# A two-layer decoder trunk: loads of the weight sums queued at other places, accumulation banks exchanged, early squares on ScalarE

## The chip, the cores and the metric

The kernel runs as one program on one core of a Trainium2 chip. The metric is the device time of one execution in microseconds (us). A core has a matrix engine (TensorE; PE in the profile, its weight loads PEld), a vector engine (VectorE; DVE), a scalar engine (ScalarE; ACT), a general engine (GpSimd; POOL), and an engine that mostly issues transfers (SyncE; SP). Each works through a queue of its own in order; where one needs another's result its instruction waits on a semaphore, and all that stands behind it in that queue waits too. SBUF is the on-chip memory. PSUM holds the results of matmuls, in banks that another engine must copy out before PE can write them again.

## The reference

The input is 1024 positions by 1024 features in float32. Two layers follow one another; each adds an attention block and an MLP to the stream. Cut to what matters:

```python
for i in range(DEPTH):                       # DEPTH = 2
    hn = rmsnorm(x, attn_norm_g[i])
    if i % 2 == 0:
        mix, q_cross = mla_mixer(hn, positions, ...)      # 12 heads, low-rank q and kv
    else:
        mix, q_cross = swa_mixer(hn, positions, ...)      # window of 128, 12 heads
    cross = memory_cross_attention(q_cross, mem_n, w_mem_kv[i])   # 4 heads
    x = x + jnp.concatenate([mix, cross], axis=-1) @ w_o[i]
    x = x + squared_relu_mlp(rmsnorm(x, mlp_norm_g[i]), mlp_w_up[i], mlp_w_down[i])
return rmsnorm(x, final_norm_g)

def squared_relu_mlp(h, w_up, w_down):
    a = jax.nn.relu(h @ w_up)
    return (a * a) @ w_down
```

## The kernel before

**Products.** Every large product is made from float32 numbers split in two: `split` (L96 to L104) has ACT round a tile to its high part `hi` (L99, or L103 with a gain) and DVE subtract it for the low part `lo` (L100, or L104). A product is then three matmuls, high by high, high by low and low by high. The output projections and the MLP also use a seven-product scheme on 2 by 2 blocks: sums of blocks are multiplied, in the products p = 1 to 7, in place of eight block products. So DVE and ACT have splits and block sums to make while PE multiplies.

**The order.** The program is written as one long function whose stages run through generators; `next(...)` advances one of them by a step at a place chosen by hand. A scheduler then orders each engine's queue within that frame, and pools of SBUF hand memory on: a tile that gets memory of an earlier tile waits for its last users. SP's queue carries nearly all transfers, so a transfer waits for those ahead of it too.

**The weight sums.** `wo_sums` (L594) makes, for a layer, sums of the blocks of `w_o` that products 5, 7, 6 and 4 of its output projection need, and stores them in DRAM (`wt_5h`, `wt_5l` and so on). The unit is a set n of four 128 by 256 tiles, of which there are eight a layer. `load(n)` issues the loads; four instructions on DVE (L620 to L623) make the sums in place; `put` splits one sum (L99, L100) and stores high and low part (L610). `run` is the generator, with two steps a set; `step` is the number of sets that have buffers. In layer 0 the first four sets use one set of buffers; sets 4 to 7 use the pool `wop` with 24 tiles: four sets of four, and eight tiles for high parts. All their loads are issued at once (L695), and the sums run in the loop over t that makes the values (`values_of`, L701) and, through `crossing`, the cross attention. `wop` is released (L831) before the tiles of the first heads are opened (`hb`, with the constant rows `kh` and `kl` that POOL writes in `head_ones`, L754 and L755), and before the loop over j that makes the keys (`pskn`) and the loads `wr` of the query weights (L526). In layer 1 two sets have buffers (tile `f1`, named `fb` in the trace), the high parts lie in query tiles (`q1`), and the sums run in the jobs n = 4 to 9 that make the queries. Directly after the last job's sums the first window scores (`s_qk`, L2062) use `f1` again.

**Cross attention.** Its scores are `pscx` (L376), maxima are taken on DVE (L423), the exponentials on ACT (L425, tile `cps`), reciprocals on DVE (L426), scaling on POOL (L428); PE transposes (`pscT`, L388), DVE and ACT copy (L392, L394), and PE multiplies (`psco`, L403).

**The output projection.** `wo_phase` (L1218) runs products 1, 5, 6, 3, 2, 7, 4 in four steps each on two groups of four banks, Y (`pswy`) and Z (`pswz`). One group is made of two double banks (`ps2`), the other of four single ones (`ps1`). In layer 0 the last attention head's result `pso` is still in PSUM when it begins, and ACT copies it out (L1032).

**The MLP.** `mlp` (L1425 on) makes the hidden blocks. `load_raw` loads a block row i of the up weights in two halves (tiles `mr` or `d`, L1443), ACT scales them (L1416), DVE makes block sums (L1459 to L1462), `prep_w` and `prep_x` split weights and input, PE multiplies (`psu`, `psv`, L1520 to L1522). `evac` copies out: for products 2, 7 and 3 DVE adds a saved product (L1572) and `square` makes relu(a)·a in one DVE instruction (L1551); sums of the squared blocks follow (L1582 to L1584), and `write` stores them. `xT_` transposes the input (`psT_m`, L1345) while the first rows i = 0 and 1 begin.

## Time and profile before

| | us |
|---|---|
| median of 3 runs | 2135.39 |
| lowest, highest | 2134.42, 2136.19 |
| the profiled execution, its own time | 2133.98 |
| its span in the profile | 2131.8 |

| stage, us from the start of the span | length | PE busy | DVE busy | ACT busy |
|---|---|---|---|---|
| 0 to 206: norms, input products, cross attention, first sums | 206 | 185.53 | 144.73 | 115.09 |
| 206 to 455: queries, layer 0's heads | 249 | 246.41 | 190.56 | 172.17 |
| 455 to 545: layer 0's output projection | 90 | 87.51 | 70.64 | 63.34 |
| 545 to 1128: layer 0's MLP | 583 | 574.32 | 419.69 | 271.97 |
| 1128 to 1345: layer 1's input products, cross attention, sums | 217 | 205.75 | 138.77 | 108.36 |
| 1345 to 1505: layer 1's windows and output projection | 160 | 158.94 | 135.24 | 129.51 |
| 1505 to 2131: layer 1's MLP, last norm | 626 | 611.34 | 447.74 | 289.02 |

The profile is of one execution, read by a hardware profiler. Its times are counted from the start of the span. A row of the timeline reads: start, duration, engine, line, operation, tiles written and read, shapes, and in brackets the time for which the engine was idle before it, and the instruction that ended this. Rows with x2 or more are runs of equal instructions put together. A row of the windows reads: the stretch and its length, then busy time and number of instructions of PE, PEld, DVE, ACT and POOL, the TensorE clock that was granted as a share of full speed (PEclk), the busy share of the DMA engines and GB/s. SPq rows are SP's issues of transfers. Times of PE overlap a little, as matmuls are pipelined: what counts there is the distance from start to start.

### The profile page before, as it was taken

The page shows a single profiled execution, that of the slowest core. Times are in us where ns is not written, and L with a number is a line of the kernel's source. Part 1 is how long each engine was busy: PE and PEld are TensorE (multiplying, and loading weights), DVE is VectorE, ACT ScalarE, POOL GpSimd, SP SyncE. Part 2 cuts the span into 40 slices and gives each one's busy share as a digit, 9 for nine tenths or more (in the row PEclk, how much of TensorE's full clock was granted, in tenths as well). Part 3 has the DMA queues.
Part 4 walks back from the last instruction along what each step waited for, and adds up shares of the span by engine and source line. Part 5 has one row for each costly group of instructions (what it writes and reads, how often), then busy time and mean ns, then how long its engine had stood idle before and what let it go on. Part 6 is the DMA issues. An engine that isn't in the chain of part 4 may idle for free.

```text
span 2131.8 us, 29731 instructions
## 1 busy us (share of the span) xinstructions
PE 2069.8 (97%) x9832; PEld 1691.2 (79%) x9832; DVE 1547.4 (73%) x3011; ACT 1149.5 (54%) x2504; POOL 163.6 (8%) x224
## 2 busy tenths in 40 slices
PE   7999999999999999999999998999999999999998
PEld 6887778778778888788888876778788878788887
DVE  7667688876977776886557557797987776976565
ACT  5556477867754453444445544777754443444452
POOL 0003100001000000000001241531000000000000
PEclk9999999999999999999999999999999999999999
DMA  8523224257254446954433226137254446954442
GB/s 268 163 62 117 60 61 120 69 164 244 84 174 150 144 142 213 324 170 144 148 119 94 75 77 207 44 121 260 89 168 163 142 132 226 324 160 152 120 119 89
DMA packets 209796, 314.43 MB, mean 147 GB/s; under 512 B 21629, under 2 KB 101994, under 8 KB 209642
## 3 DMA queue, kind: packets, MB, share of 16 engines
q1 hardware_dynamic: 196960, 293.63, 43.2%
q0 software_dynamic: 4016, 13.12, 1.8%
q10 hardware_dynamic: 8666, 5.80, 0.9%
q8 instruction: 77, 1.26, 0.3%
q14 instruction: 77, 0.63, 0.1%
HBM read 206.34 MB, written 93.63 MB: 141 GB/s over the span
## 4 chain that ended last, share of the span: by engine, by line
PE 67%; DMA 11%; DVE 11%; ACT 5%; issue 3%; SPq 1%; POOL 1%; DVEq 0%; ACTq 0%; POOLq 0%
PE psy L1857 5%; PE psy L1859 5%; PE psy L1858 5%; PE psz L1858 4%; PE psz L1859 4%; PE psz L1857 4%; DMA mr<-in_mlp_w_up_dram 4%; PE pss L947 4%; PE pso L989 4%; DMA d<-in_mlp_w_up_dram 3%; PE psu L1520 3%; PE psu L1522 2%; PE psu L1521 2%; PE psv L1522 1%; PE psv L1521 1%
## 5 line engine op out<-in xcount | busy, mean ns | idle before, releaser
L1416 ACT ACTIVATE mr<-mr,gcol 128x256 f32<-128x256 f32 (+1 forms) x160 | 68.0, 480 | 80.7 <-DMA mr<-in_mlp_w_up_dram 69.2
L1416 ACT ACTIVATE d<-d,gcol 128x256 f32<-128x256 f32 x128 | 57.8, 500 | 87.4 <-DMA d<-in_mlp_w_up_dram 73.8
L1857 PE MATMUL psy<-g 128*128 128x512 f32 x256 | 99.9, 390 | 0.0
L1858 PE MATMUL psy<-g 128*128 128x512 f32 x256 | 99.6, 389 | 0.0
L1859 PE MATMUL psy<-g 128*128 128x512 f32 x256 | 99.3, 389 | 0.0
L99 ACT ACTIVATE g<-i 128x512 fp32r<-128x512 f32 x79 | 49.6, 628 | 88.2 <-PE psz L1858 45.4
L100 DVE TENSOR_TENSOR g<-i,g 128x512 fp32r<-128x512 f32 x79 | 55.8, 706 | 50.1 <-ACT g L99 50.0
L99 ACT ACTIVATE uh<-i 128x512 fp32r<-128x512 f32 x66 | 41.6, 631 | 86.4 <-PE psy L1858 40.7
L968 ACT ACTIVATE p<-pss 128x512 f32<-128x512 f32 x108 | 63.6, 593 | 42.6 <-PE pss L947 42.1
L99 ACT ACTIVATE i<-mr 128x512 fp32r<-128x512 f32 x78 | 49.0, 629 | 69.5 <-PE psz L1858 20.4
L100 DVE TENSOR_TENSOR pl<-p,ph 128x512 fp32r<-128x512 f32 (+1 forms) x96 | 61.7, 652 | 25.6 <-ACT ph L99 25.0
L821 DVE TENSOR_REDUCE m<-psx 128x1 f32<-128x128 f32 (+5 forms) x96 | 70.3, 749 | 11.3 <-PE psx L817 11.1
L100 DVE TENSOR_TENSOR uh<-i,uh 128x512 fp32r<-128x512 f32 x66 | 45.5, 690 | 45.3 <-ACT uh L99 45.2
L1857 PE MATMUL psz<-g 128*128 128x512 f32 x192 | 74.7, 389 | 0.0
L1858 PE MATMUL psz<-g 128*128 128x512 f32 x192 | 74.7, 389 | 0.0
L1859 PE MATMUL psz<-g 128*128 128x512 f32 x192 | 74.7, 389 | 0.0
L100 DVE TENSOR_TENSOR i<-mr,i 128x512 fp32r<-128x512 f32 x78 | 53.6, 687 | 22.0 <-ACT i L99 21.6
L99 ACT ACTIVATE ph<-p 128x512 fp32r<-128x512 f32 (+1 forms) x96 | 56.4, 599 | 1.3
L1859 PEld LDWEIGHTS psy<-g 128*128 128x128 f32 x256 | 48.1, 188 | 10.0
L1857 PEld LDWEIGHTS psy<-g 128*128 128x128 f32 x256 | 48.1, 188 | 9.9
L1738 DVE TENSOR_TENSOR mqf<-mqq,mqf 128x512 f32<-128x512 f32 x64 | 43.1, 686 | 17.7 <-DMA mqq<-in_mlp_w_down_dram 17.5
L1858 PEld LDWEIGHTS psy<-g 128*128 128x128 f32 x256 | 48.1, 188 | 9.9
(709 smaller groups left out, 6984.5 us busy)
## 6 DMA issues: line engine op xcount, KB each, us to landing
i<-hd SPq DMA_DIRECT2D x154, 256.0 KB
hd<-uh SPq DMA_DIRECT2D x76, 256.0 KB
hd<-ul SPq DMA_DIRECT2D x76, 256.0 KB
mr<-in_mlp_w_up_dram SPq DMA_DIRECT2D x36, 512.0 KB
hd<-x SPq DMA_DIRECT2D x72, 256.0 KB
mr<-hd SPq DMA_DIRECT2D x70, 256.0 KB
d<-in_mlp_w_up_dram SPq DMA_DIRECT2D x32, 512.0 KB
mqq<-in_mlp_w_down_dram SPq DMA_DIRECT2D x32, 512.0 KB
```

What stands on the lines that cost most here:

```text
L99: r = nc.scalar.activation(hi, src, AF.Copy)
L100: nc.vector.tensor_tensor(lo, src, f32(hi), ALU.subtract)
L821: nc.vector.reduce_max(m8s[h][:, i : i + 1], ps[:, c], axis=AX, negate=True)
L947: return lambda: nc.tensor.matmul(o, a, b, skip_group_check=True, **kw)
L989: mms.append(lambda: nc.tensor.matmul(o, a, b, skip_group_check=True, **kw))
L1416: nc.scalar.activation(w[:, k, :], w[:, k, :], AF.Copy, scale=g_mlp[layer][:, k0 + k : k0 + k + 1])
L1520: nc.tensor.matmul(ps, wh[:, k, :], xh[:, k, :], start=p in (1, 2, 5) and k == 0, stop=False, skip_group_check=True)
L1521: nc.tensor.matmul(ps, wh[:, k, :], xl[:, k, :], start=False, stop=False, skip_group_check=True)
L1522: nc.tensor.matmul(ps, wl[:, k, :], xh[:, k, :], start=False, stop=k == 3, skip_group_check=True)
L1857: nc.tensor.matmul(ps, ah[:, j, :], bh, start=p in (1, 5, 2) and k == 0, stop=False, skip_group_check=True)
L1858: nc.tensor.matmul(ps, ah[:, j, :], bl, start=False, stop=False, skip_group_check=True)
L1859: nc.tensor.matmul(ps, al[:, j, :], bh, start=False, stop=k == NP - 1, skip_group_check=True)
```

## The change

It has six parts.

1. `run` of the weight sums: with more than one set of buffers, the next set's loads are issued at the start of the next set's sums instead of after the last `put`.
2. Layer 0's second half: the pool `wop` moves to the other side of SBUF and shrinks to 10 tiles, two sets of buffers and two tiles for high parts. The steps come at t = 1 and 2 and then once per j in the loop over the keys, and the pool is released after that loop.
3. `wo_phase` in layer 0: Z gets its double banks first, then Y its single ones.
4. `prep_x`: two splits of 128 columns become one of 256, where both are due together.
5. `square` of the rows i = 0 and 1: Relu and then Square on ACT, in place of the one instruction on DVE.
6. Layer 1: the sums' first loads are issued at job 3 instead of 4.

```diff
@@ -616,6 +616,8 @@
             if step == 1:
                 yield
             for n in ns:
+                if step > 1 and n > ns[0] and n - 1 + step in ns:
+                    load(n - 1 + step)
                 s = sets[n % step]
                 V(s[0], s[1], s[0], ALU.subtract)
                 V(s[1], s[2], s[1], ALU.subtract)
@@ -628,8 +630,8 @@
                 yield
                 put(n, 2)
                 put(n, 3)
-                if n + step in ns:
-                    load(n + step)
+                if step == 1 and n + 1 in ns:
+                    load(n + 1)
                 yield
                 if step == 1:
                     yield
@@ -689,10 +691,10 @@
 
     kvp = pool("kvp")
     v = kvp.tile([P, NT, H * 64], F32, name="v")
-    wop = pool("wop")
-    wos = wop.tile([P, 24, 256], F32, name="wos")
-    wos = [wos[:, i, :] for i in range(24)]
-    summing = wo_sums(0, range(4, 8), [wos[i : i + 4] for i in range(0, 16, 4)], wos[16:])
+    wop = pool("wop", "right")
+    wos = wop.tile([P, 10, 256], F32, name="wos")
+    wos = [wos[:, i, :] for i in range(10)]
+    summing = wo_sums(0, range(4, 8), [wos[0:4], wos[4:8]], wos[8:])
     next(summing)
     cpT = quad_tile("q0", "cpT0")
     cstp = pool("cstp", "right")
@@ -712,7 +714,7 @@
         if t == 3:
             a_cT(NT - 1)
         values_of(t)
-        for _ in range(2 if t > 1 else 0):
+        if 0 < t < 3:
             next(summing, None)
     for _ in crossing:
         pass
@@ -828,7 +830,6 @@
     kn = [kq[j // 4][:, j % 4, :] for j in range(6)]
     qr = [kq[1][:, 2, :], kq[1][:, 3, :], raw_tile([P, S], "qr2")]
     krs = raw_tile([32, S], "krs")
-    wop.release()
     hb = pool("hb")
     head_bufs(hb, 0)
     head_ones(0)
@@ -843,6 +844,10 @@
              [(wkn[kt][0][:, j * P : (j + 1) * P], wkn[kt][1][:, j * P : (j + 1) * P], [(ckh[:, kt, s], ckl[:, kt, s]) for s in halves]) for kt in range(2)])
         nc.vector.tensor_copy(kn[j][:, 0:512], ps[:, 0:512])
         nc.scalar.activation(kn[j][:, 512:1024], ps[:, 512:1024], AF.Copy)
+        next(summing, None)
+    for _ in summing:
+        pass
+    wop.release()
     wu2 = pool("wu2", "right")
     wqn = rows(wpair(wu, 2, 768, "wqn", "a"), 2) + rows(wpair(wu2, 1, 768, "wqn2", "c"), 1)
     loading = load_cols(mla_w_uq[0], 3, 96, [(wqn, 0, 64)], g_q, wu2)
@@ -1289,7 +1294,10 @@
                 return [ps[j // 2][:, (j % 2) * 512 : (j % 2) * 512 + 512] for j in range(4)]
             return [ps1(f"psw{nm}{layer}_{j}") for j in range(4)]
 
-        Y, Z = banks("y", layer == 1), banks("z", layer == 0)
+        if layer:
+            Y, Z = banks("y", True), banks("z", False)
+        else:
+            Z, Y = banks("z", True), banks("y", False)
         res = {1: (Y, a1), 5: (Z, a5), 6: (Y, u2), 3: (Z, u2), 2: (Z, a1), 7: (Y, a5), 4: (Y, c21)}
 
         def mm(n, j):
@@ -1502,6 +1510,10 @@
         def prep_x(p, cols=range(4)):
             for j in cols:
                 c = slice(j * P, (j + 1) * P)
+                if p != 6 and j < 2 or len(cols) == 4:
+                    if j % 2:
+                        continue
+                    c = slice(j * P, (j + 2) * P)
                 src = m.t2[j] if p == 6 else xr[{5: 0, 7: 1, 4: 2, 3: 3}[p]][:, :, c]
                 hi, lo = [v[:, :, c] for v in X[p]]
                 split(src, hi, lo)
@@ -1547,7 +1559,11 @@
 
         hs = {}
 
-        def square(a):
+        def square(a, i=2):
+            if i < 2:
+                nc.scalar.activation(a, a, AF.Relu)
+                nc.scalar.activation(a, a, AF.Square)
+                return
             V.scalar_tensor_tensor(a, a, 0.0, a, ALU.max, ALU.mult)
 
         def write(p, i, a):
@@ -1570,7 +1586,7 @@
             e, sp = {2: (11, 1), 7: (22, 5), 3: (21, 6)}[p]
             hs[(i, e)] = h = h_next()
             V.tensor_tensor(h, ps, s_of.pop((i, sp)), ALU.add)
-            square(h)
+            square(h, i)
             if p == 2:
                 write(1, i, h)
             elif p == 7:
@@ -2103,10 +2119,12 @@
             for t in range(NT):
                 dts[t] = dist_tile(t)
         for i in range(2):
+            if n == 3 and not i:
+                quarters, wos = [f1[:, i_ // 4, (i_ % 4) * 256 : (i_ % 4) * 256 + 256] for i_ in range(8)], []
+                summing = wo_sums(1, range(8), [quarters[0:4], quarters[4:8]], wos)
+                next(summing)
             if n == 4 and not i:
-                quarters = [f1[:, i_ // 4, (i_ % 4) * 256 : (i_ % 4) * 256 + 256] for i_ in range(8)]
-                wos = [f32(q1[10 + i_ // 4][:, (i_ % 4) * 256 : (i_ % 4) * 256 + 256]) for i_ in range(8)]
-                summing = wo_sums(1, range(8), [quarters[0:4], quarters[4:8]], wos)
+                wos += [f32(q1[10 + i_ // 4][:, (i_ % 4) * 256 : (i_ % 4) * 256 + 256]) for i_ in range(8)]
             for _ in range(2 if n > 3 else 0):
                 next(summing, None)
             if n + 1 == len(jobs):
```

How the queues change is shown at three places, without times. The first is PE's queue where layer 0's last head (`pso`, L989) ends and the output projection begins; `wob` and `woa` are split weights and input, and brackets name the engines that an instruction waits for. Before:

```order
L1300 MATMUL pswy_0_5082<-wob_4796,woa_8_4940 128x512
L1301 MATMUL pswy_0_5082<-wob_4796,woa_8_4940 128x512
L1302 MATMUL pswy_0_5082<-wob_4796,woa_8_4940 128x512
L1300 MATMUL pswy_1_5083<-wob_4796,woa_8_4940 128x512 [waits PE_49,Activation_49]
L1301 MATMUL pswy_1_5083<-wob_4796,woa_8_4940 128x512
L1302 MATMUL pswy_1_5083<-wob_4796,woa_8_4940 128x512
L1300 MATMUL pswy_2_5084<-wob_4796,woa_8_4940 128x512
```

and now:

```order
L1308 MATMUL pswy_0_5084<-wob_4796,woa_8_4940 128x512 [waits PE_49]
L1309 MATMUL pswy_0_5084<-wob_4796,woa_8_4940 128x512
L1310 MATMUL pswy_0_5084<-wob_4796,woa_8_4940 128x512
L1308 MATMUL pswy_1_5085<-wob_4796,woa_8_4940 128x512
L1309 MATMUL pswy_1_5085<-wob_4796,woa_8_4940 128x512
L1310 MATMUL pswy_1_5085<-wob_4796,woa_8_4940 128x512
L1308 MATMUL pswy_2_5086<-wob_4796,woa_8_4940 128x512
```

The first matmul on the second bank waited for ACT; now the first of the group waits for PE's own earlier work, and none of these rows for ACT. The order of the matmuls is the same.

The second place is DVE's queue in layer 0's cross attention, between the maxima for the second and the third block of positions (`cst_1`, `cst_2`); `wos` rows are the weight sums and their splits, and `qc` rows splits of the queries. Before:

```order
L423 TENSOR_REDUCE cst_1_1733<-pscx_1_1724 128x4
L340 SCALAR_TENSOR_TENSOR qc_88<-psct_0_1665,qc_88 64x128
L622 TENSOR_TENSOR wos<-wos 128x256
L100 TENSOR_TENSOR wos<-wos 128x256
L340 SCALAR_TENSOR_TENSOR qc_88<-psct_0_1665,qc_88 64x128
L623 TENSOR_TENSOR wos<-wos 128x256
L100 TENSOR_TENSOR wos<-wos 128x256
L340 SCALAR_TENSOR_TENSOR qc_88<-psct_0_1665,qc_88 64x128
L100 TENSOR_TENSOR wos<-wos 128x256 x2
L423 TENSOR_REDUCE cst_2_1750<-pscx_2_1741 128x4
L426 RECIPROCAL cst_1_1733<-cst_1_1733 128x4
```

and now:

```order
L709 COPY v<-psv_1_1681 128x384
L423 TENSOR_REDUCE cst_1_1705<-pscx_1_1696 128x4
L340 SCALAR_TENSOR_TENSOR qc_88<-psct_0_1657,qc_88 64x128
L423 TENSOR_REDUCE cst_2_1722<-pscx_2_1713 128x4
L340 SCALAR_TENSOR_TENSOR qc_88<-psct_0_1657,qc_88 64x128
L392 COPY cpT_1567<-pscT_0_1_1736 128x4x128
L340 SCALAR_TENSOR_TENSOR qc_88<-psct_0_1657,qc_88 64x128
L426 RECIPROCAL cst_1_1705<-cst_1_1705 128x4
```

The six `wos` rows between the two maxima are gone from there. In SP's queue eight loads of `wos` instead of 16 stand at the front and the other eight stand among the stores, in twos or singly; the last six stores stand behind `k<-krs` and ahead of the `wr` loads, where none did. On POOL the two MEMSETs of `kh` and `kl` stand ahead of the first L428 instead of between the sixth and the seventh, and wait for PE and POOL instead of eight transfers. The first load of `wos` waits for PE, ACT, POOL and a transfer, where it waited for PE and a transfer.

The third place is DVE's queue in layer 0's early MLP. First the splits of `mqf`, before:

```order
L1462 TENSOR_TENSOR i_0_65_5899<-mr_59_5821,i_0_64_5898 128x512
L1551 SCALAR_TENSOR_TENSOR uh_62_5885<-uh_62_5885 128x512
L100 TENSOR_TENSOR mqf_0_56_5818<-i_0_52_5810,mqf_0_56_5818 128x4x128
L100 TENSOR_TENSOR mqf_0_56_5818<-i_0_60_5836,mqf_0_56_5818 128x4x128
L100 TENSOR_TENSOR mqf_0_56_5818<-i_0_61_5867,mqf_0_56_5818 128x4x128
```

and now:

```order
L1470 TENSOR_TENSOR i_0_65_5900<-mr_59_5821,i_0_64_5899 128x512
L100 TENSOR_TENSOR mqf_0_56_5818<-i_0_52_5810,mqf_0_56_5818 128x4x128
L100 TENSOR_TENSOR mqf_0_56_5818<-i_0_60_5836,mqf_0_56_5818 128x4x128
L100 TENSOR_TENSOR mqf_0_56_5818<-i_0_61_5867,mqf_0_56_5818 128x4x128
L100 TENSOR_TENSOR i_0_69_5932<-i_0_64_5899,i_0_68_5931 128x512
```

The square (L1551) ahead of the three splits is gone. A little later, `d<-mr` is the split that is the last to read the tile `mr` that the next load overwrites; before:

```order
L100 TENSOR_TENSOR i_0_69_5931<-i_0_71_5965,i_0_68_5930 128x512
L1572 TENSOR_TENSOR ul_85_6089<-psu_0_5841,d_0_53_5815 128x512
L100 TENSOR_TENSOR x_0_84_6042<-d_0_66_5910,x_0_84_6042 128x512
L100 TENSOR_TENSOR x_0_84_6042<-i_0_65_5899,x_0_84_6042 128x512
L1551 SCALAR_TENSOR_TENSOR ul_85_6089<-ul_85_6089 128x512
L100 TENSOR_TENSOR d_0_72_5970<-mr_59_5821,d_0_72_5970 128x512
L100 TENSOR_TENSOR d_0_73_5975<-d_0_67_5911,d_0_73_5975 128x512
L100 TENSOR_TENSOR i_0_79_5991<-mr_86_6095,i_0_78_5990 128x512
```

and now:

```order
L100 TENSOR_TENSOR i_0_69_5932<-i_0_71_5965,i_0_68_5931 128x512
L100 TENSOR_TENSOR d_0_72_5970<-mr_59_5821,d_0_72_5970 128x512
L100 TENSOR_TENSOR x_0_84_6030<-d_0_66_5911,x_0_84_6030 128x512
L100 TENSOR_TENSOR x_0_84_6030<-i_0_65_5900,x_0_84_6030 128x512
L1588 TENSOR_TENSOR ul_85_6077<-psu_0_5841,d_0_53_5815 128x512
L100 TENSOR_TENSOR d_0_73_5975<-d_0_67_5912,d_0_73_5975 128x512
L100 TENSOR_TENSOR i_0_79_5987<-mr_86_6084,i_0_78_5986 128x512
```

The split `d<-mr` stands four rows earlier, ahead of the two `x` splits and L1588 (L1572 before), and the square is gone. On ACT the pairs of Relu (L1564) and Square (L1565) stand among splits and scalings. SP's queue has both `mr` loads ahead of the `d` load, where `d` and a store stood between them. Layer 1's MLP changes in the same way. In layer 1's weight sums SP's rows and their waits are the same as before, from the first load to the last store; on DVE and ACT a split of `q` and one of a sum have changed places in two of the sets.

## The prediction

> **What bounds the kernel now.** I read the page's busy shares and chain first, then the timeline of PE with its waits, then the other engines at each wait.
>
> ```profile
> PE 2069.8 (97%) x9832; PEld 1691.2 (79%) x9832; DVE 1547.4 (73%) x3011; ACT 1149.5 (54%) x2504; POOL 163.6 (8%) x224
> PE 67%; DMA 11%; DVE 11%; ACT 5%; issue 3%; SPq 1%; POOL 1%; DVEq 0%; ACTq 0%; POOLq 0%
> ```
>
> PE is busy for 2069.8 of 2131.8 us. No edit takes a matmul out, so a gain can only come from PE's 62 idle us and from stretches in which its clock is low. The idle stretches that lie at an edit are these (start, duration, instruction, and in brackets the wait before it and who ended it):
>
> ```profile
> 156.28 1.09 PE L388 MATMUL pscT<-ident,cps 128*128 128x128 f32 x8 [1.16 <-POOL cps L428]
> 161.08 0.39 PE L376 MATMUL pscx<-kmh,qc 128*128 128x256 f32 x1 [1.62 <-ACT cps L425]
> 164.35 1.97 PE L388 MATMUL pscT<-ident,cps 128*128 128x128 f32 x8 [2.06 <-POOL cps L428]
> 177.99 1.08 PE L403 MATMUL psco<-cpT,vm 128*64 128x256 f32 x8 [1.50 <-DVE cpT L392]
> ...
> 457.06 0.60 PE L1300 MATMUL pswy<-wob,woa 128*128 128x512 f32 x1 [1.88 <-ACT fa L1032]
> ...
> 557.22 0.50 PE L1521 MATMUL psu<-mqf,i 128*128 128x512 f32 x1 [1.35 <-DVE mqf L100]
> 588.38 0.50 PE L1522 MATMUL psv<-mqq,i 128*128 128x512 f32 x1 [1.92 <-DVE i L100]
> ...
> 1332.93 0.47 PE L2062 MATMUL psw<-kh,q 128*128 128x128 f32 x1 [8.89 <-DVE fb L2067]
> ...
> 1546.18 0.50 PE L1522 MATMUL psv<-mqq,i 128*128 128x512 f32 x1 [1.32 <-DVE i L100]
> ```
>
> They sit in four stages: layer 0's cross attention beside its weight sums, the start of its output projection, the first products of each MLP, and layer 1's key products with the largest wait of all. I price the edits stage by stage, against this execution's own time, 2133.98 us (span 2131.8 and 2.2 around it). The median of the runs shown, 2135.39, is 1.4 higher.
>
> **Banks of layer 0's output projection.**
>
> ```profile
> 454.78 0.40 PE L1302 MATMUL pswy<-wob,woa 128*128 128x512 f32 x1
> 458.31 0.63 PE L1300 MATMUL pswy<-wob,woa 128*128 128x512 f32 x1
> 458.74 0.63 PE L1301 MATMUL pswy<-wob,woa 128*128 128x512 f32 x1
> 463.32 0.39 PE L1302 MATMUL pswy<-wob,woa 128*128 128x512 f32 x1
> 463.55 0.39 PE L1300 MATMUL pswy<-wob,g 128*128 128x512 f32 x1
> ...
> 456.42 0.59 ACT L1032 ACTIVATE fa<-pso 64x512 f32<-64x512 f32 x1
> ...
> 457.00:458.00 1.00, 0.94 (x3) 0.74 (x4) 1.00 (x3) 0.98 (x3) 0.00 (x0) 0.65 1.03 392
> 458.00:460.00 2.00, 2.00 (x6) 1.54 (x5) 2.00 (x5) 0.79 (x3) 0.00 (x0) 0.50 0.68 214
> 463.00:487.00 24.00, 24.00 (x108) 19.87 (x107) 22.49 (x36) 15.29 (x34) 0.00 (x0) 1.00 0.95 323
> ```
>
> After three matmuls PE waits for ACT's last copy out of the last head's bank; the windows' PEclk column then reads 0.65 and 0.50, and starts lie 0.43 us apart instead of 0.23. From 454.78 to 463.55 stand 22 starts; at 0.23 they take 5.0 us, and they took 8.77. So 3.8 us are lost: 1.9 of waiting, and 1.9 of low clock. In the changed order the second product's first matmul has lost its wait for ACT. What is late next is the DMA section behind: its share is 0.95 from 463 to 487, its transfers hang on the end of the last head, not on PE, and a PE that runs 3.8 us ahead may find the weight-sum tiles of product 6 late. PE is 24.00 of 24.00 busy there, so the slack is unknown; bounds of the edit are −3.8 and 0. I take **−3.0**, near the row of the wait.
>
> The Trainium skill, "TensorE: Matmul & The Clock Gate", section "Part 1: The HAM clock gate", says that the array falls to half clock after an idle window of about 3.4 us. The rows show half clock behind a wait of 1.88 (457.06), and none behind 1.92 (the window 570 to 600, quoted below, reads 1.00). By the page's rule a wait this short is not the cause, and the low clock stays: −1.9 instead of −3.8, a rival below.
>
> **The early MLP.** Six squares a layer go from DVE to ACT.
>
> ```profile
> 554.67 0.69 DVE L1551 SCALAR_TENSOR_TENSOR uh<-uh 128x512 f32<-128x512 f32 x1
> 555.27 1.89 DVE L100 TENSOR_TENSOR mqf<-i,mqf 128x512 fp32r<-128x512 f32 x3
> ...
> 570.92 0.68 DVE L100 TENSOR_TENSOR i<-i,i 128x512 fp32r<-128x512 f32 x1
> 574.28 0.69 DVE L100 TENSOR_TENSOR d<-mr,d 128x512 fp32r<-128x512 f32 x1
> 583.43 0.69 DVE L1459 TENSOR_TENSOR i<-mr,mr 128x512 f32<-128x512 f32 x1 [2.12 <-ACT mr L1416]
> 587.65 0.68 DVE L100 TENSOR_TENSOR i<-mr,i 128x512 fp32r<-128x512 f32 x1
> ...
> 574.99 0.37 SPq L1443 DMA_DIRECT2D mr<-in_mlp_w_up_dram  x1
> ...
> 581.69 1.71 ACT L1416 ACTIVATE mr<-mr,gcol 128x256 f32<-128x256 f32 x4 [2.45 <-DMA mr<-in_mlp_w_up_dram]
> 585.55 0.58 ACT L1563 ACTIVATE x<-psu 128x512 f32<-128x512 f32 x1
> ...
> 570.00:600.00 30.00, 27.75 (x120) 21.84 (x119) 26.57 (x44) 16.32 (x35) 0.00 (x0) 1.00 0.59 193
> ```
>
> DVE loses 6 × 0.60 = 3.6 us a layer (554.67 to 555.27), ACT gains 12 × 0.58 = 7.0. In the window DVE is busy 26.57 of 30 and ACT 16.32, so ACT has room on average. The merged splits have half the instructions over the same elements; I take nothing for them.
>
> At 557.22 PE waits for `mqf`. One square stands right before the three `mqf` splits: −0.6. At 588.38 PE waits for the split of 587.65, seven DVE instructions behind L1459, which waited 2.12 for ACT's scaling of `mr`, and that for a DMA issued at 574.99. This load waited until DVE's `d<-mr` at 574.28 had freed the buffer. In the changed order `d<-mr` stands right behind `i<-i,i` (570.92), so near 571.5, and SP has the second `mr` load ahead of the `d` load. It is issued some 3 us earlier, and the wait of 1.92 goes. Sum −0.6 −1.9 = **−2.5** in layer 0, bounds 0 and −3.3 (both waits gone, 1.35 and 1.92). Layer 1 has the same code and a wait of 1.32 at 1546.18; **−1.5** (the 1.32 and a little at its `mqf`), bounds 0 and −2.5.
>
> What hides the squares is ACT's room. If it fails, DVE, which stands in order, waits for a square in front of the sums of L1582 to L1584; that is a rival.
>
> **Layer 0's sums, second half.**
>
> ```profile
> 146.92 0.22 POOL L304 TENSOR_TENSOR fa<-fa,rb 128x16 f32<-128x16 f32 x1
> ...
> 182.84 0.95 POOL L754 MEMSET kh<- 1x1024 f32 x1 [2.42 <-DMA wt_4l<-wos]
> ...
> 156.43 1.21 DVE L423 TENSOR_REDUCE cst<-pscx 128x4 f32<-128x1024 f32 x1
> 161.02 1.22 DVE L423 TENSOR_REDUCE cst<-pscx 128x4 f32<-128x1024 f32 x1
> 190.48 0.56 DVE L707 COPY v<-psv 128x384 f32<-128x384 f32 x1 [1.40 <-PE psv L121]
> ...
> 189.82 6.34 SPq L526 DMA_DIRECT2D wr<-in_mla_w_uq_dram  x5
> ...
> 148.00:183.00 35.00, 28.66 (x198) 25.61 (x197) 31.92 (x65) 27.11 (x92) 11.62 (x7) 0.95 0.43 142
> 163.00:168.00 5.00, 3.65 (x20) 3.43 (x22) 4.75 (x7) 3.90 (x15) 3.28 (x2) 0.66 0.31 103
> ```
>
> From 148 to 183 DVE is busy 31.92 of 35 and PE idles 6.3: the softmax's maxima (L423) and copies queue between the sums on DVE. In the changed order the third maximum stands two rows behind the second, with only one `qc` split between, where now 4.6 us and six sum instructions lie between them (156.43 to 161.02). That is the chain to the waits of 1.62 and 2.06 and to the low clock of 163 to 168 (0.66, worth about 5 × 0.34 = 1.7). The memsets lose their wait for the stores (2.42 of POOL) and stand ahead of the first scaling by L428. On the other side, the first load of `wos` now also waits for POOL and ACT, so it cannot start before POOL's last rotation ends, at 147.1 (146.92 + 0.22), and DVE's sums may stand waiting for loads. The bounds: all waits and the low clock gone, −6.3 −1.7 = −8.0; or DVE held at the sums, +3 (two maxima of 1.2 and a copy stuck behind late loads). I take **−2.5**, about the wait of 2.06 and a share of the clock.
>
> **Layer 1's sums.** The rows of SP, with their waits, are the same before and after, and DVE and ACT swap one pair of rows in two products that end well before 1332.93. I take **0**, bounds ±0.7 (one instruction of DVE).
>
> Sum: −3.0 −2.5 −1.5 −2.5 = −9.5, so 2124.5 against this execution, and with the median's 1.4 on top **2126** us.
>
> **The rivals.**
> *The low clock or the DMAs keep what the bank swap wins.* The low clock comes anyway (by its rule above), or product 6's tiles are late: −1.9 or less instead of −3.0, and if DVE's waits in the MLP stay too (its `mr` load could be bound by the DMA engines), −1.9 −2.5 = −4.4 at best: 2131 to 2134. For it speaks the share of 0.95, against it that only 1.9 to 3.8 us of lead are in question.
> *Layer 1's sums do finish earlier.* Then 8.89 and the low clock behind it go: the window from 1333 to 1338 reads
>
> ```profile
> 1333.00:1338.00 5.00, 5.00 (x15) 4.23 (x16) 2.04 (x15) 2.83 (x14) 2.67 (x4) 0.51 0.00 0
> ```
>
> which is 5 × 0.49 = 2.4 more: 2126 − 11 = 2115. Against it: the queue's rows don't move. That the change does not do there what its words say is my forecast.
> *Slower: DVE stands behind ACT's squares.* ACT does Relu and Square (2 × 0.58) where DVE needed 0.60, and an ACT run of scaling (1.71 at 581.69) can stand ahead of them. At two places in each layer (the rows of L1582 to L1584) DVE needs a square one or two rows after its input is made; a place costs 1.16 − 0.60 = 0.6 us, and with such a run ahead 2.3. Four places at 2.3 are 9.2; the MLP's own 4.0 are then not won, and one wait of PE that brings the low clock adds 1.9: 2126 + 9.2 + 4.0 + 1.9 = 2141. It makes the kernel slower than before once a place costs more than (9.5 − 4.0) / 4 = 1.4 us. Against it: ACT is busy only 16.32 of 30.
> *The late stores hold the query weights.* Six stores of the last sum now stand ahead of the `wr` loads (189.82). They can go only when DVE's last splits are done, which stand right ahead of the last copy of `v`, at 190.48 now. Six issues of 0.4 (0.37 at 574.99) from 191 end at 193.4, 3.6 us later than the loads start now, and PE shows no wait at the query products that follow, so part of it is slack: +1 to +4, or 2127 to 2130.
>
> **How the numbers follow.** About 0.2% (4.3 us) is what a measurement of this kernel can tell from no change. The forecast, 2120 to 2131, gets 0.60; the kept gain 0.15; layer 1 acting 0.06; the slower case 0.09; the query weights 0.10. The range reaches from 2117 to 2136: a part of the layer 1 case and the slower case are left out. Faster by over 0.2% (below 2131.1) are the forecast, layer 1 and half of the query weights, 0.60 + 0.06 + 0.05 = 0.71; within 0.2% are the kept gain, the rest of the query weights and a little of the slower case, 0.21; slower 0.08.
>
> **What would show it.** The swap: no wait before the second product's matmul at the head's end, PEclk 1.00 behind it, no wait in the section of product 6. MLP: no wait for `i` at 588, the second `mr` issued near 572, ACT's squares in no release of a PE wait. Sums: waits in 148 to 183 down from 6.3 to about 4; the first `wos` load near 141 or 147. Layer 1: the wait of 8.9 still there. The prediction is wrong if PE's idle total falls by less than 4 us, or if a new wait names a square or a `wr`.

## The result, and the profile after

| | us |
|---|---|
| before, median of the runs timed beside the change | 2135.69 (2132.02 to 2139.53, 22 runs) |
| the change, median | 2131.55 (2127.12 to 2137.0, 22 runs) |
| ratio | 0.9981, 95% interval 0.9974 to 0.9989 |
| forecast | 2126.0, range 2117 to 2136 |

The change is faster by 4.1 us (2135.69 − 2131.55), where 9.4 were forecast (2135.4 − 2126.0): the sign and the range held, the size was under half. Timed twice more, each time beside other runs of the kernel before (e10 and e16 below), the change came out at 0.9981 again.

The profiled execution took 2134.10 us (span 2132.4), which is 2.5 above its median. Its busy shares and its chain:

```profile
PE 2067.0 (97%) x9832; PEld 1689.1 (79%) x9832; DVE 1541.9 (72%) x2985; ACT 1160.4 (54%) x2514; POOL 163.2 (8%) x224
PE 66%; DMA 13%; DVE 10%; ACT 5%; issue 3%; SPq 2%; POOL 1%; DVEq 0%; ACTq 0%; POOLq 0%
```

In this execution PE is busy 2.8 us less than before and idle for 2132.4 − 2067.0 = 65.4, which is 3.4 more; DMA's share of the chain rose from 11% to 13%. By the prediction's own sign (an idle total that falls by less than 4 us) this execution says that it was wrong. But it is one execution, and a long one. In two later profiles of the same kernel (e10 and e16) PE is idle for 58.9 and 57.6, which is 3.1 and 4.4 less than before, and busy for 2068.5 and 2071.8; so neither the rise of the idle time nor the fall of the busy time belongs to the change. What the profiles share is where the waits lie. The timeline of PE, at the places of the edits:

```profile
157.32 1.07 PE L388 MATMUL pscT<-ident,cps 128*128 128x128 f32 x8 [1.67 <-ACT krT L580]
161.66 0.38 PE L376 MATMUL pscx<-kmh,qc 128*128 128x256 f32 x1 [1.01 <-ACT cps L425]
164.53 1.09 PE L388 MATMUL pscT<-ident,cps 128*128 128x128 f32 x8 [1.67 <-POOL cps L428]
177.31 1.08 PE L403 MATMUL psco<-cpT,vm 128*64 128x256 f32 x8 [0.75 <-DVE cpT L392]
188.14 1.08 PE L403 MATMUL psco<-cpT,vm 128*64 128x256 f32 x8 [2.74 <-DVE cpT L392]
...
473.80 0.50 PE L1309 MATMUL pswz<-x,g 128*128 128x512 f32 x1 [0.86 <-DMA x<-wt_5l]
483.47 0.49 PE L1308 MATMUL pswy<-x,g 128*128 128x512 f32 x1 [1.13 <-DMA x<-wt_6h]
...
558.00 0.50 PE L1533 MATMUL psu<-mqf,i 128*128 128x512 f32 x1 [0.74 <-DVE mqf L100]
...
1335.02 0.47 PE L2078 MATMUL psw<-kh,q 128*128 128x128 f32 x1 [8.43 <-DVE fb L2083]
1512.26 1.09 PE L1353 MATMUL psT_m<-ident,i 128*128 128x128 f32 x8 [2.23 <-ACT i L1342]
```

Four things are to be seen. In the cross attention the waits at 161 and 164 are shorter, the one at 157 is longer (1.67, where it was 1.16), and a new one of 2.74 stands at 188. The wait of 1.88 at the start of the output projection is gone, and two waits for weight-sum tiles have come behind it. In the MLP the wait for `mqf` fell from 1.35 to 0.74, and the waits for `i` near 588 and 1546 are gone. The wait for `f1` (8.89 before) stays at 8.43, and the one for `i` in the first products of layer 1's MLP grew from 1.02 to 2.23. Two more waits, of 1.99 and 1.65 in layer 1's cross attention (1233.55 and 1235.84), stand in this profile alone (see e10).

The windows of the same profile (start to end, length, busy time of PE, PEld, DVE, ACT, POOL, PEclk, DMA share, GB/s):

```profile
163.00:168.00 5.00, 3.46 (x30) 2.90 (x32) 4.09 (x9) 4.01 (x16) 3.51 (x2) 1.00 0.08 26
183.00:188.00 5.00, 2.39 (x15) 1.10 (x13) 5.00 (x6) 1.49 (x5) 1.67 (x1) 1.00 0.30 93
457.00:460.00 3.00, 3.00 (x15) 2.47 (x14) 3.00 (x6) 2.90 (x7) 0.00 (x0) 1.00 0.87 279
463.00:487.00 24.00, 21.83 (x92) 16.84 (x92) 20.68 (x35) 13.31 (x31) 0.00 (x0) 1.00 0.86 286
550.00:600.00 50.00, 48.36 (x215) 38.84 (x213) 45.92 (x71) 41.38 (x79) 0.00 (x0) 1.00 0.43 142
```

The low clock of 163 to 168 (0.66 before) and of 457 to 460 is gone. From 463 to 487, the stretch that the prediction calls the section of product 6, PE was busy for 24.00 of 24 and is now busy for 21.83. The stretch holds the end of product 1, product 5 and most of product 6. In the MLP's start PE does 215 matmuls in 50 us (8 of them short transposes), where the profile before has 195 in the same window.

### The profile page after: what moved, and what is told of

Read it like the earlier page. It is cut to its first block, busy times and chain, and to the rows that moved or that the text cites. A ratio compares the mean times of both kernels' runs of the same rounds, so it can differ in the third digit from the quotient of the medians.

```text
span 2132.4 us, 29711 instructions
## 1 busy us (share of the span) xinstructions
PE 2067.0 (97%) x9832; PEld 1689.1 (79%) x9832; DVE 1541.9 (72%) x2985; ACT 1160.4 (54%) x2514; POOL 163.2 (8%) x224
## 4 chain that ended last, share of the span: by engine, by line
PE 66%; DMA 13%; DVE 10%; ACT 5%; issue 3%; SPq 2%; POOL 1%; DVEq 0%; ACTq 0%; POOLq 0%
PE psy L1875 5%; PE psy L1873 5%; PE psy L1874 5%; PE psz L1875 4%; PE psz L1874 4%; PE psz L1873 4%; PE pss L952 4%; PE pso L994 4%; DMA d<-in_mlp_w_up_dram 3%; DMA mr<-in_mlp_w_up_dram 3%; PE psu L1532 3%; PE psu L1534 3%; PE psu L1533 3%; PE psv L1534 2%; PE psv L1532 2%
```

## The experiments

Line numbers shift by some lines from kernel to kernel. The runs of one batch share a chip and its runs of the kernel before: e1 to e4, e5 to e8, e9 to e12, e13 to e16, and e17 with e18. Each has 5 to 12 timed executions beside 17 to 30 of before.

### Each part alone, and the change without the sums (e1 to e4)

The bank swap alone:

```diff
-        Y, Z = banks("y", layer == 1), banks("z", layer == 0)
+        if layer:
+            Y, Z = banks("y", True), banks("z", False)
+        else:
+            Z, Y = banks("z", True), banks("y", False)
```

> Before, with the bank swap of layer 0's output projection alone. Theory A (the swap's gain is given back to the weight-sum loads behind it): the wait of 1.88 us at the head's end and the low clock are gone, new waits for wt_5 or wt_6 tiles of 1 to 3 us stand in the same section, and the time falls by 0.5 to 2 us. Theory B (the swap keeps its gain): the time falls by 3 to 4 us and no new wait for a DMA stands there. Theory C (the low clock comes anyway): PEclk near 0.5 for 2 to 4 us at the start of the section.

Measured: 2134.26 against 2134.20, ratio 1.0 (0.9991 to 1.0009). Its wait of 1.88 is gone, and the timeline of PE shows new ones behind it:

```profile
474.69 0.50 PE L1304 MATMUL pswz<-x,g 128*128 128x512 f32 x1 [0.25 <-DMA x<-wt_5l]
478.85 0.47 PE L1303 MATMUL pswz<-x,g 128*128 128x512 f32 x1 [1.37 <-DMA x<-wt_5h]
485.72 0.50 PE L1303 MATMUL pswy<-x,g 128*128 128x512 f32 x1 [0.72 <-DMA x<-wt_6h]
```

From the first matmul of the projection to the end of the wait for `i` with which product 2 begins lie 48.31 us before (454.32 to 502.63) and 49.06 here (457.69 to 506.75). The swap is worth nothing that this measurement can tell.

The MLP alone, parts 4 and 5:

```diff
         def prep_x(p, cols=range(4)):
             for j in cols:
                 c = slice(j * P, (j + 1) * P)
+                if p != 6 and j < 2 or len(cols) == 4:
+                    if j % 2:
+                        continue
+                    c = slice(j * P, (j + 2) * P)
...
-        def square(a):
+        def square(a, i=2):
+            if i < 2:
+                nc.scalar.activation(a, a, AF.Relu)
+                nc.scalar.activation(a, a, AF.Square)
+                return
```

> Before, with the early squares on ScalarE and the merged splits alone. Theory A (the MLP edits win in both layers, and part is given back in layer 1's cross attention, where an in-order wait of DVE for a load of its weight sums holds PE): the two MLP stages together are 8 to 10 us shorter, the time falls by 4 to 9 us, and waits of PE of 1 to 2 us before pscT stand in layer 1's cross attention in this profile. Theory B (as predicted, no giving back): the stages are 4 us shorter, the time falls by 4, and layer 1's cross attention is as before.

Measured: 2125.23, ratio 0.9961 (0.9949 to 0.9974), so 9.0 us (2134.20 − 2125.23), over twice the forecast for both layers together. The waits in layer 1's cross attention that theory A expects are not in this profile.

Layer 0's sums alone, with the changed order of loads (parts 1 and 2; part 1 also moves layer 1's later loads):

```diff
+                if step > 1 and n > ns[0] and n - 1 + step in ns:
+                    load(n - 1 + step)
...
-    summing = wo_sums(0, range(4, 8), [wos[i : i + 4] for i in range(0, 16, 4)], wos[16:])
+    summing = wo_sums(0, range(4, 8), [wos[0:4], wos[4:8]], wos[8:])
...
-        for _ in range(2 if t > 1 else 0):
+        if 0 < t < 3:
             next(summing, None)
...
+        next(summing, None)
+    for _ in summing:
+        pass
+    wop.release()
```

> Before, with layer 0's second half of the weight sums at its new place alone (parts 1 and 2). Theory A (the late sums stand on DVE ahead of the softmax's copies and are stretched by POOL's scalings): the stage from 146 us to the key products is 2 us longer, a wait of PE of 2 to 3 us ended by a cpT copy stands near 188 us, and the time rises by 1 to 3 us. Theory B (as predicted: the maxima come earlier): the stage is 2.5 us shorter and so is the time.

Measured: 2136.50, ratio 1.0011 (1.0001 to 1.0021): 2.3 slower, with a wait of 2.76 for `cpT` at 191.33, as in the change. From the first key product (`pskn`, 186.33) to the first query product (`psqr`, 215.69) PE takes 29.36 us, where it took 25.29 before (183.76 to 209.05).

The change without its parts 1, 2 and 6, so with the swap and the MLP alone (the diff is those of the first two runs):

> The change without its parts 1, 2 and 6 (weight sums as before): bank swap and MLP edits. Theory A (the sums' new place costs 2 us): faster than before by 5 to 9 us, so 2 us or more ahead of the change's own 4 us. Theory B (the sums' new place wins 2.5 us and the loss lies elsewhere): faster than before by 1 to 2 us only.

Measured: 2124.68, ratio 0.9955 (0.9943 to 0.9967): 9.5 us below before, and well below the change.

### Two causes tested (e5, e6), another queue (e7), the squares alone (e8)

The change, with the last steps of layer 0's sums held until the cross attention's last two copies (`cx_end`, one on ACT and one on DVE, L404 to L408) are done:

```diff
-        next(summing, None)
+        with tc.issue_after(cx_end[0].ins), tc.issue_after(cx_end[1].ins):
+            next(summing, None)
```

> The change, with layer 0's last three sums held on DVE and ACT until the cross attention's last copies are done. Theory A (the cost of the new place is that sums stand ahead of the softmax's copies and are stretched by POOL's scalings): no split or sum of wos takes over 0.6 us, the wait of 2 to 3 us before psco near 188 us is gone, the stage from the first pscx to the first pswy is 3 us shorter than in the change (311.3 us), and the time is 2 to 4 us below the change's. Theory B (the work is only in the way somewhere else): waits move to the key and query products (pskn, psqr, psqt), and the stage stays within 1 us of the change's.

Measured: 2128.99 against 2132.98, ratio 0.9985 (0.9976 to 0.9994). The wait of 2.74 is gone, but the timeline of PE has this one in its place:

```profile
219.60 0.69 PE L880 MATMUL psqt<-ident,fa 128*128 128x128 f32 x2 [8.39 <-POOL fa L304]
```

POOL in turn had waited for DVE's L300, which ran at 217.97: on DVE it stands behind the last splits of the sums, and it waited for their last store (`wt_4l<-wos`) to land. In this profile no sum or split of `wos` after the hold takes over 0.43, and the way from the first key product to the first query product is back at 25.10; the way from there to the first `psqt` takes 13.26, where it took 4.88. So the sums were what held the cross attention's copies, and at a later place they hold the next work that needs DVE. Neither theory came out whole: the wait went and the splits are short, but the time is not 2 to 4 us below the change's; the waits moved to the query products, but the stage from the first `pscx` to the first `pswy` is 316.7 (144.57 to 461.23), 5.4 longer than the change's. Why the time is then no longer than the change's stays open.

The swap, with the eight residual tiles of layer 0's projection set to zero by POOL in place of their loads (the residual is left out of layer 0's attention block):

```diff
             for j in range(4):
+                if layer == 0:
+                    nc.gpsimd.memset(dst[j], 0.0)
+                    continue
                 nc.sync.dma_start(out=dst[j], in_=m.x_src[r * 512 + j * P : r * 512 + j * P + P, c * 512 : c * 512 + 512])
```

> Before with the bank swap, and layer 0's loads of the residual x in the output projection left out (POOL writes zeros in their place, so layer 0's residual is left out of the output). Theory A (the section is bound by transfers, so the swap's gain was given back to late loads): the waits for wt_5 and wt_6 tiles are gone, and the section from the first pswy to the wait for i at product 7's end is 44 to 46 us instead of 48.3 to 49.1. Theory B (something else ends the section, such as DVE's evacuations): it stays at 47.5 or more.

Measured: 2127.59, ratio 0.9975 (0.9966 to 0.9984). The window of product 6, of the swap alone first and then without those loads:

```profile
463.00:487.00 24.00, 21.37 (x90) 16.28 (x89) 18.73 (x32) 11.44 (x27) 0.00 (x0) 1.00 0.84 271
```

```profile
463.00:487.00 24.00, 24.00 (x107) 19.87 (x107) 22.51 (x38) 16.92 (x38) 1.05 (x2) 1.00 0.82 262
```

and the two ends of the section without those loads:

```profile
456.21 0.39 PE L1306 MATMUL pswy<-wob,woa 128*128 128x512 f32 x1
500.00 0.46 PE L1306 MATMUL pswz<-x,g 128*128 128x512 f32 x1
```

Without the loads PE is busy all through, no wait for a weight-sum tile is left, and the section takes 43.79 us (456.21 to 500.00) instead of 49.06, as theory A has it. So the residual's loads took back the lead. Whether they did it by their bytes or by their place in SP's queue is not told apart: the DMA share is nearly the same in both windows (0.84 and 0.82), but SP issues the next load of `wt_5l` 2.7 us after the projection's first matmul (458.89) here, and 12.2 us after it in the swap (469.84 against 457.69), right behind a residual load. The old banks without these loads were not run.

The fourth run with layer 1's low-part stores on POOL's queue:

```diff
-            for d_, t_ in zip(wts[layer][(5, 7, 6, 4)[i]], (hi, lo)):
-                nc.sync.dma_start(out=d_[:, k, c * 256 : c * 256 + 256], in_=f32(t_))
+            for d_, t_, q_ in zip(wts[layer][(5, 7, 6, 4)[i]], (hi, lo), (nc.sync, nc.gpsimd if layer else nc.sync)):
+                q_.dma_start(out=d_[:, k, c * 256 : c * 256 + 256], in_=f32(t_))
```

> The change without its parts 1, 2 and 6, and with layer 1's stores of the low parts of the weight sums issued by POOL's queue instead of SP's. Theory A (the wait of 8 us before layer 1's first window scores is set by SP's issues: eight stores and the loads of the next set, one after the other): the wait falls below 3 us and the time by 6 to 9 us more, to 2116 to 2119 where the run before is 2134. Theory B (the wait is set by DVE's or the transfers' own time): the wait stays above 6 us.

Measured: 2130.84, ratio 0.9988 (0.9979 to 0.9996). The wait for `f1` shortened to 5.07, between the two theories, but two new ones came ahead of it:

```profile
1291.46 0.47 PE L109 MATMUL psf<-xnh,wf 128*128 128x512 f32 x1 [2.90 <-DVE q L340]
1308.17 0.47 PE L109 MATMUL psf<-xnh,wf 128*128 128x512 f32 x1 [3.01 <-DVE q L340]
1333.51 0.48 PE L2073 MATMUL psw<-kh,q 128*128 128x128 f32 x1 [5.07 <-DVE fb L2078]
```

At the first of them DVE had waited 3.60 for a store (`wt_5h<-q`, at 1289.05). Layer 1's sums stand in a loop of loads, DVE and stores; a faster end of it was paid for in its middle.

Part 5 alone, the squares on ACT without the merged splits (the second half of the MLP diff above):

> Before, with the early squares on ScalarE alone (splits not merged). Theory A (the squares carry the MLP's gain): faster by 6 to 9 us, as the MLP edits together were by 9. Theory B (the merged splits share it): faster by 3 to 5 us.

Measured: 2138.19, ratio 1.0027 (1.0017 to 1.0038): 5.2 slower, where both theories expected a gain. The timeline of PE:

```profile
557.97 0.50 PE L1521 MATMUL psu<-mqf,i 128*128 128x512 f32 x1 [0.74 <-DVE mqf L100]
587.74 0.50 PE L1520 MATMUL psv<-mqf,x 128*128 128x512 f32 x1 [0.78 <-ACT x L99]
590.48 0.50 PE L1522 MATMUL psv<-mqq,i 128*128 128x512 f32 x1 [2.01 <-DVE i L100]
```

The wait for `mqf` is down by the 0.6 of one square, as forecast. The wait of 1.92 at 588 is still there, as 2.01.

### The merged splits alone, the change again, layer 1's sums held (e9 to e12)

Part 4 alone (the first half of the MLP diff):

> Before, with the merged splits alone (squares stay on DVE). Theory A (the merged splits win because they change DVE's and SP's order, d<-mr earlier and the second mr load ahead of the d load, so the waits near 588 us and at its twin in layer 1 go): faster by 5 to 8 us, the wait at 588 is gone, the wait of 1.35 for mqf near 557 stays. Theory B (both edits are needed together, as DVE is only then free): within 2 us of before.

Measured: 2128.31 against 2132.93, ratio 0.9981 (0.9971 to 0.9991). The wait at 588 is gone without a single square on ACT. The timeline shows why; the issues of SP and one row of DVE, first with the squares alone, then with the merged splits alone:

```profile
573.51 0.38 SPq L1443 DMA_DIRECT2D d<-in_mlp_w_up_dram  x1
574.83 0.34 SPq L1558 DMA_DIRECT2D hd<-ul  x1
575.26 0.39 SPq L1443 DMA_DIRECT2D mr<-in_mlp_w_up_dram  x1
...
583.59 0.69 DVE L1459 TENSOR_TENSOR i<-mr,mr 128x512 f32<-128x512 f32 x1 [2.40 <-ACT mr L1416]
```

```profile
567.27 6.13 SPq L1443 DMA_DIRECT2D mr<-in_mlp_w_up_dram  x2
574.21 0.37 SPq L1443 DMA_DIRECT2D d<-in_mlp_w_up_dram  x1
...
572.30 0.68 DVE L100 TENSOR_TENSOR d<-mr,d 128x512 fp32r<-128x512 f32 x1
...
578.75 0.69 DVE L1459 TENSOR_TENSOR i<-mr,mr 128x512 f32<-128x512 f32 x1 [0.23 <-ACT mr L1416]
```

With the merged splits `d<-mr` stands at 572.30 (574.28 before), the second `mr` load is the end of a pair that closes at 567.27 + 6.13 = 573.40, and L1459 runs at 578.75 in place of 583.43.

The change unchanged, on this chip:

> The change once more, for a second profile and time beside the next runs. Theory A (the two waits of PE of 2.0 and 1.7 us with low clock in layer 1's cross attention, 6.4 us in all, come in some executions of this order and not in others): the profile may show them or not, the median lies 3 to 5 us below before. Theory B (they belong to the change): they stand in this profile again.

Measured: 2128.88, ratio 0.9981 (0.9972 to 0.9989). The change's first profile has waits of 1.99 and 1.65 in layer 1's cross attention (1233.55 and 1235.84), which this one has not.

The change, and then the fourth run, each with layer 1's sums held on DVE until the cross attention's last copy:

```diff
             for _ in range(2 if n > 3 else 0):
-                next(summing, None)
+                with tc.issue_after(cx_end[0].ins):
+                    next(summing, None)
```

> The change, with layer 1's sums held on DVE until its cross attention's last copy is done, so no sum stands ahead of the copies. Theory A (an in-order wait of DVE for a load of the sums costs the change some 3 us in the middle of its executions): 2 to 4 us faster than the change once more, no wait for a load on DVE in layer 1's cross attention. Theory B (that wait was one profile's accident): as fast as the change within 1 us.

> The change without its parts 1, 2 and 6, and with layer 1's sums held on DVE in the same way. Theory A: as fast as without the hold or up to 2 us faster, 9 to 12 us below before. Theory B (the hold delays the chain of stores that ends at the wait of 8 us before the first window scores): the wait grows to 9 us or more and the time is 1 to 3 us longer than without the hold.

Measured: 2128.55, ratio 0.9979 (0.997 to 0.9989), as the change; and 2123.83, ratio 0.9958 (0.9941 to 0.9974), as the fourth run. The change's waits at 1233 stand in its first profile alone, not in e10 nor in e16, and holding the sums there gains nothing.

### All on one chip (e13 to e16)

The earlier runs put the merged splits at 4.6 us and both MLP parts at 9.0, on different chips. Four of the kernels were timed together, each with the same edit as above: the merged splits, both MLP parts, the fourth run, the change.

> Merged splits of the early MLP alone, beside the next three on one chip. Theory A (the squares help only behind the merged splits): 4 us below before and 3 to 5 above the kernel with both MLP edits. Theory B (the squares on ScalarE do nothing once the splits are merged, the difference between the two earlier runs was one of chips): equal to the kernel with both within 1 us.

> Both MLP edits, nothing else. A: 8 us below before. B: as the merged splits alone within 1 us, 4 to 6 below before.

> Both MLP edits and the bank swap, the weight sums as before. If the swap is worth nothing: equal to the run with both MLP edits within 1 us. If the swap is worth its forecast 3 us: 3 below it.

> The change as it is. If the moved sums of layer 0 cost 2 to 5 us: that much above the run without them (the one before in this call). If they cost nothing and only the chips differed: equal to it within 1 us.

Measured, against 2132.85:

| | us | ratio, 95% interval |
|---|---|---|
| merged splits | 2124.70 | 0.9958 (0.9946 to 0.9970) |
| both MLP parts | 2123.76 | 0.9953 (0.9941 to 0.9965) |
| both, and the swap | 2123.53 | 0.9953 (0.9941 to 0.9965) |
| the change | 2128.71 | 0.9981 (0.9968 to 0.9993) |

Here the merged splits hold nearly all of the MLP's gain (8.2 of 9.1); the squares add 0.9 and the swap 0.2, neither of which this measurement can tell from nothing. The moved sums cost 5.2 (2128.71 − 2123.53). That the merged splits gave 4.6 on one chip and 8.2 on another, with intervals that do not meet, was not explained; in the two profiles layer 0's MLP, from its first `psu` to layer 1's first `pscx`, takes 656.2 and 655.1, and layer 1's, from its first `psu` to PE's end, 624.5 and 625.2, so the difference is not seen there. Runs are therefore compared within a batch.

### Which layer's sums cost it (e17, e18)

The change with layer 1's sums as before, and the fourth run with layer 1's moved loads (part 6, and part 1, which moves layer 1's later loads too):

```diff
-                if step > 1 and n > ns[0] and n - 1 + step in ns:
+                if layer == 0 and n > ns[0] and n - 1 + step in ns and step > 1:
                     load(n - 1 + step)
...
-                if step == 1 and n + 1 in ns:
-                    load(n + 1)
+                if (step == 1 or layer) and n + step in ns:
+                    load(n + step)
...
-            if n == 3 and not i:
...
             if n == 4 and not i:
```

> The change with layer 1's sums as before (part 6 gone, and part 1 for layer 0 alone). Theory A (all of the 5 us that the moved sums cost lies in layer 0): as the change, 3 to 5 us below before, and 4 to 6 above the other run of this call. Theory B (about half lies in layer 1): 6 to 7 below before.

> Both MLP edits, the bank swap, and part 1 with part 6 in layer 1; layer 0's sums as before. A: 9 us below before, as without any moved sums. B: 6 to 7 below before; then a wait in layer 1 between 1195 and 1345 is new or longer.

Measured, against 2132.70: 2128.26, ratio 0.9981 (0.9971 to 0.999), and 2124.88, ratio 0.9967 (0.9956 to 0.9977). With layer 0's part alone the gain is the whole change's, 4.4; with layer 1's alone it is 7.8, which lies between the two theories, and the two runs are 3.4 apart. So layer 0's part costs most of the 5. Some 1.3 to 1.7 may be layer 1's (the gain without any moved sums was 9.1 to 9.5 on other chips), which the intervals leave open. The profile shows no such cost: from layer 1's first `pscx` to its first window score take 120.3 us here, and 120.4 and 119.7 in the two profiles of the fourth run's kernel (e4 and e15).

## Why the forecast was right and wrong

**The bank swap: forecast −3.0, shown 0.** The first half of the step was right to the row: the wait went, PEclk reads 1.00 from 457 to 460, and PE reaches the next product 10.92 us after the first matmul (456.20 to 467.12), where it took 14.67 (454.32 to 468.99), so the lead is the 3.8 forecast. The step that failed is the slack behind it. I had seen the DMA share of 0.95 and named late tiles as the risk, but took a value near the wait all the same, as PE was busy for 24.00 of 24. A busy PE showed that it was not waiting yet, not that it had room. The swap alone gave the lead back in full, in waits for tiles of products 5 and 6, and without the residual's loads the section was 5.3 shorter (43.79 against 49.06): what holds it back is when the weight-sum tiles land.

**The low clock as part of that price.** The rival that the low clock stays was wrong: in the profiles of the swap alone and of the change it is gone with its wait. But counting 1.9 us for it was wrong too. The same wait of 1.88 stands in the runs without the swap. No low clock follows it in either run of the merged splits alone nor in the first run with both MLP parts, and in the second run with both it comes 1.0 later. The timeline of PE, of the first run of the merged splits and then of the second run with both MLP parts (PEclk from 458 to 463 reads 1.00 and 0.66):

```profile
458.42 0.50 PE L1300 MATMUL pswy<-wob,woa 128*128 128x512 f32 x1 [1.88 <-ACT fa L1032]
458.76 0.40 PE L1301 MATMUL pswy<-wob,woa 128*128 128x512 f32 x1
458.99 0.39 PE L1302 MATMUL pswy<-wob,woa 128*128 128x512 f32 x1
```

```profile
458.10 0.49 PE L1300 MATMUL pswy<-wob,woa 128*128 128x512 f32 x1 [1.88 <-ACT fa L1032]
...
458.89 0.40 PE L1300 MATMUL pswy<-wob,woa 128*128 128x512 f32 x1
459.13 0.53 PE L1301 MATMUL pswy<-wob,woa 128*128 128x512 f32 x1
459.45 0.63 PE L1302 MATMUL pswy<-wob,woa 128*128 128x512 f32 x1
...
462.43 0.49 PE L1300 MATMUL pswy<-wob,woa 128*128 128x512 f32 x1
```

And it did not matter: with full clock and the wait (the first of these two) the section took 48.20 (455.68 to 503.88), with low clock (before) 48.31.

**The MLP: forecast −4.0, shown −9.** The mechanism was right in both its halves, the wait for `mqf` shorter by one square and the `mr` load issued earlier, so that the wait of 1.92 went. Two steps were not. First, I took nothing for the merged splits, for their elements stay the same, and read the new order as the squares' work. It is theirs: the squares alone leave SP's order and the wait as they were, and the merged splits alone remove it and win 4.6 or 8.2. Second, the size. From layer 0's first `psu` to layer 1's first `pscx` PE takes 655.6 us on average over the 13 profiles with both MLP parts (654.6 to 657.3), and 659.9 over the four with the old ones (658.6 to 661.2): 4.3 less, where I had counted only the two large waits (2.5). From layer 1's first `psu` to PE's end it is 624.2 (622.8 to 625.8) against 628.5 (627.6 to 629.9): 4.3 less, where I had a guess by likeness of 1.5. The longer wait for `i` (2.23) is in the latter already. Which smaller waits make up the rest was not followed.

**The rival with DVE behind ACT's squares** did not happen in the change. The squares alone did make the kernel slower, by 5.2, but not in the way that I had told: in that profile no instruction of DVE waits for a square, and it is ACT that waits for DVE's sum ahead of a Relu, for 2.11 at 576.92 and 2.28 at 1537.29. ACT's scaling of `mr`, which had waited for its load (1.71 from 581.85), did stand ahead of four instructions of squares, from 583.46 on, and ACT's next split (`i<-mr`) behind them, at 585.55, where it stood at 583.70 before. On DVE all six sums of squares stand between L1459 (583.59) and the split for which PE waits (589.74, ten rows on instead of seven). That these rows cost all of the 5.2 is not shown: that profile has 2.4 of it in layer 0's MLP (662.35 against the 659.9 above) and 1.3 in layer 1's (629.8 against 628.5). With the merged splits the load comes early, and the loss is gone: it was decided by part 4, which I had put at nothing.

**Layer 0's sums: forecast −2.5, shown +2.3 alone and about +5 in the whole.** This is the term whose sign failed. What I forecast of the front is there: the first `wos` load at 147.10, the waits of 1.62 and 2.06 down to 1.01 and 1.67, the clock at 1.00. Yet PE's busy time from 148 to 183 is 28.67 against 28.66: next to nothing was gained even there, as waits of 0.3 to 0.9 came at other rows. Behind it lies the cost, which I had named only as a bound (copies stuck behind the sums, +3). The timeline of DVE, POOL and SP in the change:

```profile
172.05 2.00 DVE L624 TENSOR_TENSOR wos<-wos 128x256 f32<-128x256 f32 x1
...
182.50 0.43 DVE L625 TENSOR_TENSOR wos<-wos 128x256 f32<-128x256 f32 x1
182.84 2.45 DVE L100 TENSOR_TENSOR wos<-wos 128x256 fp32r<-128x256 f32 x2
185.22 0.54 DVE L709 COPY v<-psv 128x384 f32<-128x384 f32 x1
185.68 0.67 DVE L836 COPY krs<-krT 32x1024 f32<-32x1024 f32 x1
186.28 1.21 DVE L423 TENSOR_REDUCE cst<-pscx 128x4 f32<-128x1024 f32 x1
187.42 0.67 DVE L392 COPY cpT<-pscT 128x512 f32<-128x512 f32 x1
188.01 0.40 DVE L100 TENSOR_TENSOR wos<-wos 128x256 fp32r<-128x256 f32 x1
...
190.06 2.06 DVE L100 TENSOR_TENSOR wos<-wos 128x256 fp32r<-128x256 f32 x1 [0.28 <-ACT wos L99]
...
171.88 1.90 POOL L428 TENSOR_TENSOR cps<-cps,cst 128x1024 f32<-128x1024 f32 x1 [1.80 <-DVE cst L426]
...
182.72 1.95 POOL L428 TENSOR_TENSOR cps<-cps,cst 128x1024 f32<-128x1024 f32 x1 [1.81 <-DVE cst L426]
189.95 1.89 POOL L428 TENSOR_TENSOR cps<-cps,cst 128x1024 f32<-128x1024 f32 x1 [5.28 <-PE pscT L388]
...
193.81 3.61 SPq L526 DMA_DIRECT2D wr<-in_mla_w_uq_dram  x4
```

DVE is never idle from 183 to 188, and PE is busy for 2.39 of 5. The copy of `v`, a maximum and the copy of `cpT`, for which PE waits 2.74, stand behind two splits that take 2.45 in place of 2 × 0.41. In the kernel before, DVE had no sums left here (the copy of `v` stood at 182.25). The sums were moved out of a place with cover into one without, and the run that held them longer (e5) shows the same from the other side. The price is the same in every profile: from the first key product to the first query product PE takes 28.6 to 29.4 in the six with the sums moved and not held, and 25.0 to 26.3 in the 13 with the sums as before, while the stretches just ahead of it and just behind are 0.7 and 0.8 shorter. In all, from the first `pscx` to layer 0's first head (`pss`), that is 112.9 against 110.5 on average, 2.4 longer. It agrees with what the sums cost alone, 2.3 (0.2 to 4.5 by the interval). In the whole change they cost 5.2 and 4.7 in two batches (the latter with layer 1's sums held in both kernels); where the other 2 to 3 lie stays open.

**Layer 1's sums: forecast 0, shown 0 to 1.5 slower.** The wait of 8.9 stayed, as forecast. **The late `wr` loads** came as their rival said, 4.0 late (193.81 against 189.82), and no PE wait names them: its mechanism was right and its price nothing.

Summed by what the runs showed, 0 − 9 + 5 = −4 makes the 4.1 measured. The sign came out as forecast because an error of 5 in one term and errors of 3 and 7.5 in two others partly offset each other, and that is luck. Luck, too, is how near the time lies to the first rival's 2131 to 2134: its lead lost to late tiles was real, but its MLP that wins less was the opposite of what the runs showed. The fastest version found is the change without parts 1, 2 and 6, or its MLP parts alone: 2123.5 to 2125.2 in four runs, 0.9953 to 0.9961 of before.

## What to carry to other kernels

A PE that never waits in a section with the DMA engines at 0.95 has no proven slack: ask when the loads behind it are issued, and when they can land, before counting a lead as a gain. Merging instructions over the same elements is not neutral where a scheduler fills the order: see what moves ahead of what, and which load that frees. Before moving work on a busy engine to a later place, look at what stands behind it there and at what its neighbour engine does at that time.

## What the hardware showed

**DVE beside POOL.** A split or sum of 128 by 256 on DVE that takes 0.41 took 2.00 and 2.06 where it met POOL's scaling of `cps` (1.90 and 1.89), and ended just after it (190.06 + 2.06 = 192.12, against 189.95 + 1.89 = 191.84). The Trainium skill, "SBUF — State Buffer", section "SBUF: two separate sides", says that a DVE instruction with two SBUF inputs and a GpSimd instruction that reads SBUF exclude one another for a whole instruction; the trace agrees. The forecast gave this no price at the sums' new place.

**The low clock.** One wait of 1.88, at the same instruction, brought half clock from its first matmul (before, 457.06 to 460.6), from 1.0 later (459.13 to 462.43), or not at all. Each time it lasts some 3.4 us. The Trainium skill, "TensorE: Matmul & The Clock Gate", section "Part 1: The HAM clock gate", says that the gate judges in windows of about 3.4 us that run free of the program; the lengths agree, but the page's whole idle window of that length was not needed here.
